# Row-wise division by the sum of absolute values: loads and stores of all tiles issued from one queue in a fixed order

## The chip, the cores and the metric

The kernel runs on one core of a Trainium2 chip. The metric is the time on the device in microseconds (us), the median of several executions of the same compiled program. The engines named here are VectorE (DVE in the profile), ScalarE (ACT), GpSimd (POOL) and SyncE (SP). SyncE does no arithmetic; it issues transfers (DMAs) and waits on semaphores. ScalarE computes and can issue transfers too. The transfers themselves are carried out by 16 DMA engines, whichever engine issued them.

## The reference

The input is a tensor of 32 x 512 x 1024 float32 numbers. Each row of 1024 is divided by the sum of its absolute values:

```python
def reference(x: np.ndarray) -> np.ndarray:
    sums = np.sum(np.abs(x), axis=-1, keepdims=True)
    return (x / (sums + 1e-8)).astype(np.float32)
```

There are 16384 rows, 67.11 MB in and the same amount out. No number is read twice and there is nothing for TensorE to do.

## The kernel before

The 16384 rows are spread over the 128 partitions of the on-chip memory, so each partition holds 128 rows in all. They are worked on in eleven tiles. Ten tiles have 12 rows in each partition (128 x 12 x 1024 numbers, 6.29 MB), and the last has 8 (4.19 MB). The list `rows` holds these sizes and `piece` gives the part of the input or output that belongs to a tile. A partition's share of a tile is contiguous in HBM, 48 KB for 12 rows and 32 KB for 8.

The tiles live in the pool `sbuf`, which has four buffers (`BUFS = 4`). Tile 4 goes into the buffer of tile 0, tile 5 into that of tile 1, and so on. The results are written over the input in the same buffer (`row` is both input and output), so a buffer is free for the next load only when the store of the tile that it held has landed.

For each tile, `normalize` does this:

- one reduction on DVE over the whole tile, giving 12 sums of absolute values for each partition (line 52);
- two small DVE instructions on these sums: adding a tiny constant (line 59) and the reciprocal (line 61);
- the scaling of the rows by the reciprocals. Most rows are scaled by one DVE multiplication (line 63). In the tiles named in the table `split`, some rows are scaled one at a time by DVE (line 70) or by ACT (line 73), to shorten the work on the first and the last tiles.

The order of the work is written out by hand: inside `tc.manual_schedule()` each engine executes its instructions in program order. The loop runs over the tiles, and for each it issues the load on SyncE's queue (line 88), the computation, and the store on ScalarE's queue (line 91). SyncE thus has only loads to issue. It runs ahead of the computation: the first four loads have free buffers and are issued at once, and each later load waits until the store of four tiles before has landed. ScalarE has only stores to issue, each as soon as both DVE and ACT are done with the tile. Loads and stores are therefore on two separate queues, and the DMA engines serve both at once.

Of the kernel before, what the change touches and what calls it, by code (L numbers as in the profile page):

```python
# [1 line left out]

# [4 lines left out]

FP32 = mybir.dt.float32
EPS = 1e-8


@with_exitstack
def kernel(
    ctx: ExitStack,
    tc: tile.TileContext,
    x: bass.AP,
    out: bass.AP,
):
    nc = tc.nc
    P = nc.NUM_PARTITIONS  # L20

    x_flat = x.flatten_outer_dims()
    out_flat = out.flatten_outer_dims()
    n, d = x_flat.shape

    R = 12
    BUFS = 4  # L30
    HEAD = 32
    per_partition = n // P
    assert n % P == 0 and (per_partition - HEAD) % R == 0
    rows = [R] * ((per_partition - HEAD) // R + 2) + [HEAD - 2 * R]

    def piece(flat, i):
        head = flat[: P * HEAD, :].rearrange("(p r) d -> p r d", p=P)
        if i < 2:
            return head[:, R * i : R * (i + 1), :]
        if i == len(rows) - 1:  # L40
            return head[:, 2 * R :, :]
        a = P * (HEAD + R * (i - 2))
        return flat[a : a + P * R, :].rearrange("(p r) d -> p r d", p=P)

    sbuf = ctx.enter_context(tc.tile_pool(name="sbuf", bufs=BUFS))
    stats = ctx.enter_context(tc.tile_pool(name="stats", bufs=len(rows)))

    def normalize(x_tile, k, kv, kt):


        s = stats.tile([P, R], FP32)
        nc.vector.tensor_reduce(  # L52
            out=s[:, :k],
            in_=x_tile[:, :k, :],
            axis=mybir.AxisListType.X,
            op=mybir.AluOpType.add,
            apply_absolute_value=True,
        )
        nc.vector.tensor_scalar_add(out=s[:, :k], in0=s[:, :k], scalar1=EPS)  # L59
        inv = stats.tile([P, R], FP32)  # L60
        nc.vector.reciprocal(out=inv[:, :k], in_=s[:, :k])  # L61
        if kv:
            nc.vector.tensor_mul(  # L63
                out=x_tile[:, :kv, :],
                in0=x_tile[:, :kv, :],
                in1=inv[:, :kv].unsqueeze(2).to_broadcast([P, kv, d]),
            )
        for r in range(kv, kv + kt):
            row = x_tile[:, r, :]
            nc.vector.tensor_scalar_mul(out=row, in0=row, scalar1=inv[:, r : r + 1])  # L70
        for r in range(kv + kt, k):
            row = x_tile[:, r, :]
            nc.scalar.activation(  # L73
                out=row,
                in_=row,
                func=mybir.ActivationFunctionType.Copy,
                scale=inv[:, r : r + 1],
            )

    last = len(rows) - 1
    split = {0: (3, 4), 1: (0, 3), 2: (0, 3), last - 1: (0, 2), last: (5, 3)}

    with tc.manual_schedule():
        for i, k in enumerate(rows):
            x_tile = sbuf.tile([P, R, d], FP32)
            nc.sync.dma_start(out=x_tile[:, :k, :], in_=piece(x_flat, i))  # L88
            kt, ks = split.get(i, (0, 0))
            normalize(x_tile, k, k - kt - ks, kt)  # L90
            nc.scalar.dma_start(out=piece(out_flat, i), in_=x_tile[:, :k, :])


# [1 line left out]
_INS = ['x']  # L95
_OUTS = [((32, 512, 1024), 'float32')]


# [23 lines left out]
```

## Time and profile before

| What | Value |
|---|---|
| median of three executions | 317.26 us (317.24 to 317.40) |
| span of the profiled execution, first to last instruction | 315.8 us |
| time outside the span, median less span | 1.46 us |
| moved by the DMA engines | 134.22 MB, 425 GB/s over the span |
| DVE busy | 261.2 us, 83% of the span |
| ACT busy | 17.4 us |
| loads, 12 rows | ten of 6144 KB, median 38.0 us from issue to landing |
| stores, 12 rows | ten of 6144 KB, median 47.4 us from issue to landing |

The profiled execution has no total time of its own beside the span on the page; what lies around the span is taken from the difference to the median of the executions without the profiler.

The page lists the busy time of each engine, the span in 40 slices, the DMA queues (q1 is SyncE's, with the loads; q10 is ScalarE's, with the stores), the chain of work that ended last, groups of instructions and the DMA issues. The busy share of the DMA engines is a mean over all 16. A view by windows gives the same numbers for any stretch of the span. In it a DMA packet counts wholly in the window in which it starts, so that in a window shorter than a packet the share can be over 1 or be 0; over long windows this evens out. A packet here is the share of one partition in one transfer: a transfer of 12 rows has 128 data packets of 48 KB, eight for each DMA engine, and each engine ends its part with one packet of a few bytes that counts up the semaphore.

### The profile page before, as it was taken

How to read it: one execution, taken by the hardware profiler on the slowest of the kernel's cores; microseconds unless marked ns; L12 is line 12 of the kernel's file. 1: busy time of each engine (PE TensorE's matmuls, PEld its weight loads, DVE VectorE, ACT ScalarE, POOL GpSimd, SP SyncE). 2: the span in 40 equal slices, each digit the busy share in tenths (PEclk: the TensorE clock that was granted, in tenths of full speed). 3: DMA queues.
4: the chain of work that ended last, by engine and by line, in shares of the span. 5: the costliest groups of instructions: out<-in, count | busy, mean ns of one | idle time of the engine just before them, and what ended most of it. 6: DMA issues, size and time to landing. Idle time of an engine off the chain costs nothing.

```text
span 315.8 us, 168 instructions
## 1 busy us (share of the span) xinstructions
DVE 261.2 (83%) x51; ACT 17.4 (6%) x16; POOL 0.2 (0%) x4
## 2 busy tenths in 40 slices
DVE  0079999999999999969996999799699969999200
ACT  0010404004000000000000000000000000201200
POOL 0000000000000000000000000000000000000000
DMA  8999999999999999999999999999999999999986
GB/s 324 473 398 448 448 361 430 405 486 405 405 486 405 405 486 411 423 467 405 448 436 411 479 405 411 473 417 405 473 417 411 467 413 450 421 442 423 473 374 282
DMA packets 3168, 134.22 MB, mean 425 GB/s; under 512 B 352, under 2 KB 352, under 8 KB 352
## 3 DMA queue, kind: packets, MB, share of 16 engines
q1 hardware_dynamic: 1584, 67.11, 49.8%
q10 hardware_dynamic: 1584, 67.11, 49.1%
HBM read 67.11 MB, written 67.11 MB: 425 GB/s over the span
## 4 chain that ended last, share of the span: by engine, by line
DVE 41%; DMA 33%; another core or an unknown queue 18%; issue 0%; SPq 0%; DVEq 0%
DVE s L52 23%; DMA x_tile<-in_x_dram 17%; DMA out_dram<-x_tile 16%; DVE x_tile L63 15%; DVE x_tile L70 1%; DVE inv L61 0%; DVE s L59 0%; SPq L88 0%; DVEq L117 0%
## 5 line engine op out<-in xcount | busy, mean ns | idle before, releaser
L52 DVE TENSOR_REDUCE s<-x_tile 128x12 f32<-128x12288 f32 (+1 forms) x11 | 138.2, 12561 | 31.5 <-DMA x_tile<-in_x_dram 31.5
L63 DVE TENSOR_TENSOR x_tile<-x_tile,inv 128x12288 f32<-128x12288 f32 (+3 forms) x10 | 113.6, 11358 | 0.5
L73 ACT ACTIVATE x_tile<-x_tile,inv 128x1024 f32<-128x1024 f32 x15 | 16.1, 1138 | 258.7 <-DVE inv L61 258.7
L70 DVE TENSOR_SCALAR x_tile<-x_tile,inv 128x1024 f32<-128x1024 f32 x8 | 5.5, 748 | 0.0
L61 DVE RECIPROCAL inv<-s 128x12 f32<-128x12 f32 (+1 forms) x11 | 2.5, 226 | 0.4
L73 ACT ACT_TABLE_LOAD x1 | 1.3, 1283 | 17.7 <-DMA x_tile<-in_x_dram 17.7
L59 DVE TENSOR_SCALAR s<-s 128x12 f32<-128x12 f32 (+1 forms) x11 | 1.9, 173 | 0.4
L106 POOL MEMSET const-bfloat16-1.0<- 128x1 bf16 x1 | 0.1, 102 | 0.0
L106 POOL MEMSET const-uint8-127<- 128x1 uint8 x1 | 0.1, 102 | 0.0
L106 POOL MEMSET const-float32-0.0<- 128x1 f32 x1 | 0.1, 99 | 0.2 <-issue 0.2
L106 POOL MEMSET const-float32-1.0<- 128x1 f32 x1 | 0.1, 99 | 0.0
## 6 DMA issues: line engine op xcount, KB each, us to landing
x_tile<-in_x_dram SPq DMA_DIRECT2D x10, 6144.0 KB, 38.0
out_dram<-x_tile ACTq DMA_DIRECT2D x10, 6144.0 KB, 47.4
x_tile<-in_x_dram SPq DMA_DIRECT2D x1, 4096.0 KB, 33.3
out_dram<-x_tile ACTq DMA_DIRECT2D x1, 4096.0 KB, 20.6
```

The lines of the kernel that those rows point to most:

```text
L52: nc.vector.tensor_reduce(out=s[:, :k], in_=x_tile[:, :k, :], axis=mybir.AxisListType.X, op=mybir.AluOpType.add, apply_absolute_value=True,)
L59: nc.vector.tensor_scalar_add(out=s[:, :k], in0=s[:, :k], scalar1=EPS)
L61: nc.vector.reciprocal(out=inv[:, :k], in_=s[:, :k])
L63: nc.vector.tensor_mul(out=x_tile[:, :kv, :], in0=x_tile[:, :kv, :], in1=inv[:, :kv].unsqueeze(2).to_broadcast([P, kv, d]),)
L70: nc.vector.tensor_scalar_mul(out=row, in0=row, scalar1=inv[:, r : r + 1])
L73: nc.scalar.activation(out=row, in_=row, func=mybir.ActivationFunctionType.Copy, scale=inv[:, r : r + 1],)
L106: nc = _bacc.Bacc("TRN2", target_bir_lowering=False, num_devices=1)
```

## The change

The stores move from ScalarE's queue to SyncE's, which now issues all 22 transfers. The order in which SyncE issues them is fixed by the program: the loads of tiles 0 to 3, the stores of tiles 0 and 1, the load of tile 4, the store of tile 2, the load of tile 5, and so on in turn, until the load of tile 10 and then the stores of tiles 8, 9 and 10. An instruction of this queue that has to wait holds up those behind it: a store waits for the computation of its tile, and a load waits for the store that frees its buffer. The tile sizes, the number of buffers, the instructions of `normalize`, their order on DVE and ACT and the bytes moved stay as they are.

```diff
     with tc.manual_schedule():
-        for i, k in enumerate(rows):
-            x_tile = sbuf.tile([P, R, d], FP32)
-            nc.sync.dma_start(out=x_tile[:, :k, :], in_=piece(x_flat, i))
-            kt, ks = split.get(i, (0, 0))
-            normalize(x_tile, k, k - kt - ks, kt)
-            nc.scalar.dma_start(out=piece(out_flat, i), in_=x_tile[:, :k, :])
+        for i in range(BUFS):
+            load(i)
+        compute(0)
+        store(0)
+        for i in range(1, n_tiles):
+            compute(i)
+            store(i)
+            if i - 1 + BUFS < n_tiles:
+                load(i - 1 + BUFS)
```

The functions it calls are new:

```diff
+    tiles = {}
+
+    def load(i):
+        x_tile = tiles[i] = sbuf.tile([P, R, d], FP32, name="x_tile")
+        nc.sync.dma_start(out=x_tile[:, : rows[i], :], in_=piece(x_flat, i))
+
+    def store(i):
+        nc.sync.dma_start(out=piece(out_flat, i), in_=tiles[i][:, : rows[i], :])
+
+    def compute(i):
+        k = rows[i]
+        kt, ks = split.get(i, (0, 0))
+        normalize(tiles[i], k, k - kt - ks, kt)
+
+    n_tiles = len(rows)
```

## The prediction

> **What bounds the kernel now.** I read the page from the top: span, busy times, the slices, then the DMA queues.
>
> ```profile
> span 315.8 us, 168 instructions
> DVE 261.2 (83%) x51; ACT 17.4 (6%) x16; POOL 0.2 (0%) x4
> ...
> DMA  8999999999999999999999999999999999999986
> ...
> DMA packets 3168, 134.22 MB, mean 425 GB/s; under 512 B 352, under 2 KB 352, under 8 KB 352
> ## 3 DMA queue, kind: packets, MB, share of 16 engines
> q1 hardware_dynamic: 1584, 67.11, 49.8%
> q10 hardware_dynamic: 1584, 67.11, 49.1%
> ```
>
> DVE has 54.6 us of idle time; the DMA engines have almost none: the two queues' shares add to 98.9% of the span. The bound is the 16 DMA engines, not DVE and not a wait. So the first question is whether they can run faster in any mix of work. I asked the view by windows for three stretches of 14.5 us: loads alone, loads and stores together, stores alone (the last load is due to have landed by 281.5, where the last reduction starts).
>
> ```profile
> core 0: us, DVE busy (x) ACT busy (x) POOL busy (x), PEclk, DMA share, GB/s
> 18.90:33.40 14.50, 14.40 (x4) 2.38 (x4) 0.00 (x0) 1.00 1.00 434
> 126.00:140.50 14.50, 12.21 (x1) 0.00 (x0) 0.00 (x0) 1.00 1.00 434
> 282.00:296.50 14.50, 11.90 (x8) 3.23 (x3) 0.00 (x0) 1.00 1.00 434
> ```
>
> All three read 434 GB/s at a share of 1.00: loads alone, stores alone and both at once run equally fast. The first window also crosses the boundary from the load of tile 1 to that of tile 2 (eight packets each, one after the other on one queue) with no loss. At 434 GB/s the 134.22 MB take 309.3 us of the 315.8. What is left, 6.5 us, is all that the DMA side has to give. It lies at the start, at one place early on, and at the end. The start and the early place:
>
> ```profile
> 0.00:1.50 1.50, 0.00 (x0) 0.00 (x0) 0.20 (x4) 1.00 0.00 0
> 1.50:2.00 0.50, 0.00 (x0) 0.00 (x0) 0.00 (x0) 1.00 4.42 1376
> ...
> 4.00:4.50 0.50, 0.00 (x0) 0.00 (x0) 0.00 (x0) 1.00 3.18 1376
> ```
>
> ```profile
> 38.00:39.00 1.00, 1.00 (x2) 0.00 (x0) 0.00 (x0) 1.00 1.71 737
> 39.00:40.00 1.00, 1.00 (x1) 0.00 (x0) 0.00 (x0) 1.00 0.11 49
> 40.00:41.00 1.00, 1.00 (x1) 0.00 (x0) 0.00 (x0) 1.00 3.08 786
> 41.00:42.00 1.00, 1.00 (x1) 0.00 (x0) 0.00 (x0) 1.00 0.00 0
> 42.00:43.00 1.00, 1.00 (x1) 0.00 (x0) 0.00 (x0) 1.00 0.00 0
> 43.00:44.00 1.00, 1.00 (x1) 0.00 (x0) 0.00 (x0) 1.00 1.70 737
> ```
>
> A packet counts where it starts. The window from 38 holds 737 GB/s x 1 us = 15 packets of 49152 bytes, so one takes 1.71 x 16 / 15 = 1.82 us, the normal packet. The window from 40 holds exactly 16 packets, one for each engine, and its share of 3.08 says that each took 3.08 us: 1.26 more than normal, on all engines. The first store was issued on ScalarE's queue at 38.67 (timeline), so this is what opening the second queue cost, once. No other full round of packets is stretched so. At the start, the first packets begin near 1.7: the window from 1.5 holds 1376 GB/s x 0.5 us = 14 of the 16, each of 4.42 x 0.5 x 16 / 14 = 2.5 us, 0.7 over normal. The account: 1.7 + 0.7 + 309.3 + 1.26 = 313.0, the mean end of the engines, and 2.8 us from there to the end of the span (the slowest engine ends about 1.4 after the mean, then the last landing and the closing semaphores).
>
> Last, the waits of SyncE and of DVE, to see what the changed order has to respect.
>
> ```profile
> SPq L88 <- DMA out_dram<-x_tile: 227.8, 7, 56.4
> ...
> DVE s L52 <- DMA x_tile<-in_x_dram: 31.5, 7, 17.6
> ```
>
> All seven later loads wait for a store to free a buffer; DVE waits 31.5 us for loads, 17.6 for the first. As the DMA engines are busy meanwhile, these waits cost nothing by themselves.
>
> **The change part by part.** Unchanged: every instruction of DVE and ACT, the bytes, and the start. The sum is made against the span of 315.8; the median is 1.46 above it, which I carry over.
>
> *Issuing.* Eleven stores leave ScalarE (0.34 us each) and are issued by SyncE beside its eleven loads (0.33 us): 22 x 0.33 = 7.3 us of issue time in 315, each while another transfer is running. At nothing, as long as the queue holds an earlier transfer for over 0.33 us. ACT's 16 instructions wait for DVE alone, so its lighter queue gains nothing.
>
> *One queue, in order.* A transfer of 12 rows takes 14.5 us of every engine alone (8 x 1.81), one of 8 rows 9.7. In order, with the first load done at 17, loads 1 to 3 end at 31.5, 46 and 60.5. The store of tile 0 is issued at 38.7 as now, but has loads 2 and 3 ahead of it: it runs 60.5 to 75, store 1 (issued 61.8) to 89.5. Load 4 waits for store 0, is issued at about 75.5 and runs 89.5 to 104. Then store 2 to 118.5, load 5 to 133, store 3 to 147.5, load 6 to 162, and in steps of 14.5 on: load 10 to 273, stores 8, 9 and 10 to 287.5, 302, 312. The question is whether each is issued in time. DVE, with 26.4 us for a full tile (12.95 + 0.4 + 12.96), ends tile 2 at 84.8 and tile 3 at 111.2 as now; load 4 is then in, so tile 4 ends at 137.6, 5 at 164, 6 at 190.5, 7 (its load in at 191) at 218, 8 (220) at 247, 9 (249) at 273.5, 10 at 287. Store 4 is issued at 137.7 and wanted at 162; store 6 at 190.5 and wanted at 220; store 10 at 287, wanted at 302. Load 4 is issued when store 0 ends, with store 1 (14.5 us) still in the queue; each later load has a load and a store ahead of it. The tightest cover is about 14 us (store 1, load 4, store 10); it would have to vanish wholly before an engine idles.
>
> *The new waits.* Behind a store that waits for DVE now stands a load. Load 7 needs store 3 (147.5); the store ahead of it, 4, is issued at 137.7. Loads 8, 9 and 10 have 12 to 16 us in hand in the same way (stores 4, 5 and 6 end at 176.5, 205.5 and 234.5; stores 5, 6 and 7 are issued at 164, 190.5 and 218), and store 5 (164) stands behind load 7 (148). Neither holds up the other. DVE waits some 1 to 2 us for each of loads 7 to 9, with over 15 us of transfers queued ahead of its stores, so at no cost.
>
> *The second queue is not opened.* The 1.26 us at 40 to 43 go if they belong to a queue that is opened while another runs; they stay if they belong to the first store as such. Between 0 and 1.26 I take the whole: from 43 on stores and loads alternate at 1.81 us a packet, so a change of direction has no price of this kind.
>
> *Changes of direction on one queue.* In one queue the order turns from loads to stores eight times and back seven times. No row shows this on one queue. From below: no gain, since no stage exceeds 434 GB/s. The nearest row for nothing is the mixed stretch, 434 GB/s with both directions on every engine. From above: 0.7 us for a packet on an empty pipeline (the start), or 1.26 (the opening): 15 x 0.7 = 10.5, 15 x 1.26 = 18.9. I take 0, because the mixed stretch has the same engines turning between packets, and differs only in which queue a packet comes from.
>
> *The end.* Stores 9 and 10 end alone in both kernels. In order, the engines may end closer together: after 14.5 us windows of loads they still start within about 0.5 us of one another, at the end they are some 1.4 apart. Between 0 and 1.4 I take 0.2.
>
> Sum: 315.8 - 1.26 - 0.2 = 314.3 of span, with 1.46 around it **315.8 us**.
>
> **Two rules of the Trainium skill.** The page "DMA: Bandwidth & Descriptors", section "Issuing engines are not separate DMA queues", says that all transfers share the same 16 engines and that several issuers only save issue time. By it alone the change is worth nothing, 317.26; the row at 40 to 43 adds a price for the second queue that the page does not have. The same page, section "Anatomy of one DMA" (for the GpSimd path), gives a fixed cost of about 2 us for each transfer, mostly the receipt of the last write. This speaks against the change: if one queue exposed it at each of 21 boundaries, the page's figure would make an estimate of 42 us more. The window of loads alone crosses such a boundary at 434 GB/s, so here it is overlapped.
>
> **The rivals.** *First, no change:* the 1.26 us belong to the first store after loads alone, and come again at 60. For it: it is seen once, at the first store, so the profile can't part the two. Against: later stores show nothing like it. Time: 317.26, less up to 0.2.
>
> *Second, slower: the turn between directions costs on one queue.* Place: the 15 turns. For it: with two queues an engine may fetch from one while it finishes the other; with one it has nothing else at the turn. Against: load follows load on one queue without a gap. Price: 0.7 each gives 317.26 - 1.26 + 10.5 = 326.5; 1.26 each gives 334.9; 0.4 each gives 322. It decides from (1.26 + 0.63) / 15 = 0.13 us a turn.
>
> *Third, the queue runs dry* because a waiting store or load stands in front. For it: SyncE's queue now mixes both waits. Against: 12 to 14 us of cover everywhere. One dry spell costs about 1.0 (issue at 0.73 to the first packet at 1.7) + 0.7; at seven loads 12 us, 328.
>
> **How the numbers follow.** What can be told from no change here is 0.2%, 0.63 us. Forecast 0.60; first rival 0.12; second 0.24; third 0.04. So faster 0.60, same 0.12, slower 0.28. The forecast's own range is 314.6 (the opening and the whole spread at the end gone: 317.26 - 1.26 - 1.4) to 316.6. The range with the others goes up to 322, the second rival at 0.4 a turn; small prices are likelier, so about half of that case, and all of the third, lie above: some 0.15 in all, with 0.03 below.
>
> **What the new profile would show.** Right: no round of 3.08 us packets near 40 or 60; one queue with some 99% of the span; 434 GB/s over windows that cross a turn (such as 82 to 111); loads landing 14 to 15 us after the transfer ahead; DVE idle moved, not gone. Wrong: packets longer than 1.82 us at each turn, at 60, 89.5, 104 and so on, or slices under 9 tenths in the middle. The prediction fails most simply if a turn on one queue costs more than 0.13 us.

## The result and the profile after

The changed kernel is slower: a median of 320.02 us (319.82 to 320.45, four runs) against 317.33 us for the kernel before beside it, a ratio of 1.0082 with a 95% interval of 1.0069 to 1.0096. I had forecast 315.8 us. The case that I had called the second rival, a cost at the turns between loads and stores on one queue, took place.

The page of the changed kernel, the lines that answer to those shown of before:

```profile
span 318.2 us, 159 instructions
DVE 261.1 (82%) x51; ACT 17.4 (5%) x16; POOL 0.2 (0%) x4
...
DMA  8999999999999999999999999999999999999994
...
DMA packets 3168, 134.22 MB, mean 422 GB/s; under 512 B 352, under 2 KB 352, under 8 KB 352
## 3 DMA queue, kind: packets, MB, share of 16 engines
q1 hardware_dynamic: 3168, 134.22, 98.3%
```

The same packets are all on one queue, the busy times of DVE and ACT are the same within 0.1 us, and no slice in the middle is under nine tenths. So no DMA engine ran dry for want of a transfer. The only slice that falls is the last, from 6 tenths to 4. Its rate on the page falls from 282 to 177 GB/s. The loss shows at the end of the span.

The waits of SyncE and of DVE:

```profile
SPq L86 <- DVE x_tile L58: 137.1, 9, 24.3
SPq L83 <- DMA out_dram<-x_tile: 93.9, 7, 17.1
...
DVE s L47 <- DMA x_tile<-in_x_dram: 28.5, 6, 17.7
```

SyncE now waits for computation and for stores, as the change says, and DVE waits for loads a little less than before (28.5 against 31.5 us). The waits are not what costs time.

The view by windows, with a packet counted where it starts, has three parts to look at. First the whole stretches, which answer to the 434 GB/s of before:

```profile
core 0: us, DVE busy (x) ACT busy (x) POOL busy (x), PEclk, DMA share, GB/s
62.00:76.50 14.50, 14.40 (x4) 1.36 (x2) 0.00 (x0) 1.00 1.00 434
82.00:111.00 29.00, 28.90 (x5) 0.00 (x0) 0.00 (x0) 1.00 1.00 432
111.00:140.00 29.00, 28.84 (x6) 0.00 (x0) 0.00 (x0) 1.00 1.00 431
140.00:169.00 29.00, 26.94 (x5) 0.00 (x0) 0.00 (x0) 1.00 1.00 432
```

Stores alone run at 434 GB/s as before. The windows that hold turns have 431 or 432 at a share of 1.00: the engines are busy, but some packets take longer. Now the first turn, from load 3 to store 0, and two packets at a later one:

```profile
58.00:59.00 1.00, 1.00 (x1) 0.00 (x0) 0.00 (x0) 1.00 2.48 688
59.00:60.00 1.00, 1.00 (x1) 0.00 (x0) 0.00 (x0) 1.00 0.36 98
60.00:61.00 1.00, 1.00 (x1) 0.00 (x0) 0.00 (x0) 1.00 0.00 0
61.00:62.00 1.00, 1.00 (x2) 0.00 (x0) 0.00 (x0) 1.00 1.71 737
...
191.50:192.30 0.80, 0.80 (x1) 0.00 (x0) 0.00 (x0) 1.00 1.54 614
```

The window from 58 holds 688 GB/s x 1 us = 14 packets, each of 2.48 x 16 / 14 = 2.83 us: the last packets of load 3, stretched by 1.0. The stretch that I had put down to the opening of the second queue is still there, 18 us later, at the first store to reach the engines. In the window from 191.5 there are 614 x 0.8 = 491 KB, ten packets, of mean 1.54 x 0.8 x 16 / 10 = 1.97 us. Two of them, on engines that are 1.3 and 1.8 us behind the median, take 2.57 and 2.59 us in the records of the packets; the other eight take the normal 1.82.

Last, the final packets of all engines, in the changed kernel and then in the kernel before:

```profile
312.00:313.00 1.00, 0.00 (x0) 0.00 (x0) 0.00 (x0) 1.00 0.53 229
313.00:314.00 1.00, 0.00 (x0) 0.00 (x0) 0.00 (x0) 1.00 0.23 98
314.00:315.00 1.00, 0.00 (x0) 0.00 (x0) 0.00 (x0) 1.00 0.23 98
315.00:316.00 1.00, 0.00 (x0) 0.00 (x0) 0.00 (x0) 1.00 0.23 98
```

```profile
312.00:313.00 1.00, 0.00 (x0) 0.00 (x0) 0.00 (x0) 1.00 0.46 197
313.00:314.00 1.00, 0.00 (x0) 0.00 (x0) 0.00 (x0) 1.00 0.16 66
314.00:315.00 1.00, 0.00 (x0) 0.00 (x0) 0.00 (x0) 1.00 0.00 0
```

These packets belong to tile 10, whose 8 rows make packets of 32 KB. Before, the last two (66 GB/s x 1 us) start between 313 and 314. After, three (98 GB/s x 1 us) still start in each microsecond up to 316. Three engines are late by some 3 us, and the kernel ends when the slowest does.

To find where these engines lost their time I joined the packets into one chain for each engine. The records don't name the engine, but a packet starts within a few nanoseconds of the end of the one before it, and eight data packets and one counting packet make up an engine's part of a transfer. Durations over the normal 1.82 us are the loss. The mean over the 16 engines in the changed kernel is 0.69 us at the start, 1.04 at the first turn (0.66 to 1.36), 0.78 at the last two packets of a load ahead of the seven later turns to a store, 0.15 at the first two packets of a load after a turn back, and nothing elsewhere. The slowest engine lost 3.06 us after the first turn. The mean end of the engines moved from 313.41 (before) to 313.96, the end of the slowest from 314.38 to 316.75. That is 2.37 us, and the span grew by 2.4. Most of the loss is thus in how far the engines end apart. The rest of this study asks what makes the late engines late.

### The profile page after: what moved, and what is told of

It reads as the page before. It is cut to its first block, busy times and chain, and to the rows that moved or that the text cites. A ratio compares the mean times of both kernels' runs of the same rounds, so it can differ in the third digit from the quotient of the medians.

```text
span 318.2 us, 159 instructions
## 1 busy us (share of the span) xinstructions
DVE 261.1 (82%) x51; ACT 17.4 (5%) x16; POOL 0.2 (0%) x4
## 4 chain that ended last, share of the span: by engine, by line
DMA 58%; DVE 33%; DVEq 0%; issue 0%; SPq 0%
DMA x_tile<-in_x_dram 32%; DMA out_dram<-x_tile 26%; DVE s L47 19%; DVE x_tile L58 12%; DVE x_tile L65 1%; DVE inv L56 0%; DVE s L54 0%; DVEq L129 0%; DVEq L58 0%; SPq L86 0%; SPq L83 0%
## 5 line engine op out<-in xcount | busy, mean ns | idle before, releaser
L47 DVE TENSOR_REDUCE s<-x_tile 128x12 f32<-128x12288 f32 (+1 forms) x11 | 138.2, 12561 | 28.5 <-DMA x_tile<-in_x_dram 28.5
```

The source lines that it names most:

```text
L47: nc.vector.tensor_reduce(out=s[:, :k], in_=x_tile[:, :k, :], axis=mybir.AxisListType.X, op=mybir.AluOpType.add, apply_absolute_value=True,)
```

## The experiments

All times are medians, and each ratio is to the kernel before on the same chip, with its 95% interval. The span and the end of the last engine are those of one profiled execution, which need not be like the median one.

| Kernel | queues | turns from loads to stores | time, us | ratio | span | last engine ends |
|---|---|---|---|---|---|---|
| before | 2 | packet by packet | 317.33 | 1 | 315.8 | 314.4 |
| changed | 1 | 8 | 320.02 | 1.0082 (1.0069 to 1.0096) | 318.2 | 316.8 |
| changed, again | 1 | 8 | 320.23 | 1.0089 (1.0074 to 1.0105) | 318.8 | 317.4 |
| pairs | 1 | 5 | 318.71 | 1.0043 (1.0027 to 1.0059) | 317.0 | 315.5 |
| stores on ScalarE | 2 | packet by packet | 317.07 | 0.9990 (0.9974 to 1.0007) | 315.0 | 313.6 |
| copy | 1 | 8 | 320.29 | 1.0091 (1.0060 to 1.0122) | 318.5 | 317.2 |
| copy, fours | 1 | 3 | 317.30 | 0.9994 (0.9976 to 1.0012) | 314.9 | 313.7 |
| copy, fours, eight engines late | 1 | 3 | 322.09 | 1.0157 (1.0143 to 1.0172) | 320.1 | 318.9 |
| halves | 1 | 8 | 320.12 | 1.0086 (1.0072 to 1.0099) | 318.0 | 316.6 |
| halves in turn | 1 | 15 | 321.87 | 1.0146 (1.0133 to 1.0159) | 319.8 | 318.4 |
| two engines late | 1 | 8 | 321.93 | 1.0142 (1.0128 to 1.0157) | 319.6 | 318.0 |
| early store | 2 | packet by packet | 317.54 | 1.0006 (0.9994 to 1.0017) | 315.0 | 313.7 |
| flat, two queues | 2 | packet by packet | 318.14 | 1.0025 (1.0009 to 1.0042) | 318.4 | 317.0 |
| flat, one queue | 1 | 8 | 320.69 | 1.0105 (1.0092 to 1.0118) | 319.2 | 317.8 |

The theory at first: on one queue, an engine that turns from a load to a store loses time, the late engines most. The rivals were the order of issue (not the queue), the waits for DVE and its traffic, and a lag that has nothing to do with turns.

### Fewer turns: pairs

```diff
-        compute(0)
-        store(0)
-        for i in range(1, n_tiles):
-            compute(i)
-            store(i)
-            if i - 1 + BUFS < n_tiles:
-                load(i - 1 + BUFS)
+        for i in range(0, last, 2):
+            compute(i)
+            store(i)
+            compute(i + 1)
+            store(i + 1)
+            for j in (i + BUFS, i + 1 + BUFS):
+                if j <= last:
+                    load(j)
+        compute(last)
+        store(last)
```

> All transfers stay on SyncE's queue, but the loads and stores after the first four loads go in pairs (two stores, two loads), so that the queue turns from loads to stores five times instead of eight, and back four times instead of seven. Turn theory (a DMA engine that turns from a load to a store on one queue loses time, the late engines most): the first turn still costs about 1.0 us on all engines, the later loss of the slowest engine (about 3.5 us in the changed kernel) shrinks to about 4/7 of it, 2.0, so 318.5 us. Rival, lag from something that does not depend on turns (number of loads, number of transfers): 320.0 as before.

318.71 us, close to the 318.5 of the turn theory, and its interval excludes the time of the changed kernel. The number of transfers, their sizes and the work are the same; only the order differs. The slowest engine lost 2.38 us after the first turn, against 3.06.

### The queue alone: stores on ScalarE

```diff
     def store(i):
-        nc.sync.dma_start(out=piece(out_flat, i), in_=tiles[i][:, : rows[i], :])
+        nc.scalar.dma_start(out=piece(out_flat, i), in_=tiles[i][:, : rows[i], :])
```

> The program order of the changed kernel is kept, only the stores go back to ScalarE's queue. Turn theory: 317.3 us, with the engines ending about 1.4 us apart. Rival, the order of issue is to blame and not the single queue: about 320.

317.07 us: with the program order of the changed kernel, and only the queue of the stores put back, the whole loss is gone. The engines end within 0.74 us of each other, closer than I expected. The order of issue by itself is out.

### No computation: copy

```diff
     def compute(i):
-        k = rows[i]
-        kt, ks = split.get(i, (0, 0))
-        normalize(tiles[i], k, k - kt - ks, kt)
+        pass
```

> The same queue and the same order of the 22 transfers as in the changed kernel, with the whole computation left out: the output is a copy of the input. Turn theory: the loss lies in the DMA engines alone, so the time stays near 320.0 (319 to 321) and stretched last packets of loads appear before every turn to a store. Rival, the waits of SyncE for DVE or the traffic of DVE and ACT in the on-chip memory cause the loss: 316.0 to 317.0, with no stretched packets after the first turn.

320.29 us, as the turn theory has it. DVE and ACT do nothing here, and SyncE waits for transfers alone, so neither their traffic nor their lateness is the cause. The loss lies in the transfers themselves.

### Fewest turns: copy in fours

```diff
-        for i in range(BUFS):
-            load(i)
...
+        for g in range(0, n_tiles, BUFS):
+            group = range(g, min(g + BUFS, n_tiles))
+            for i in group:
+                load(i)
+            for i in group:
+                store(i)
```

> As the copy, with the computation left out, but four loads and four stores in turn, so that the queue turns three times from loads to stores and twice back. Turn theory: time below the other copy by about 5/7 of the 3.5 us lost after the first turn, so about 317.5. If every turn of engines that are in step costs 1 us like the first one: three rounds of packets of about 2.8 us on all engines. Rival, turns do not matter: the same time as the other copy within 0.6.

317.30 us against 317.5 expected: 3.0 below the other copy, with all bytes on one queue. In this copy, one queue as such costs nothing, then; the turns do. In its windows, the first turn and the second:

```profile
58.00:59.00 1.00, 0.00 (x0) 1.00 2.54 737
59.00:60.00 1.00, 0.00 (x0) 1.00 0.18 49
...
172.90:174.70 1.80, 0.00 (x0) 1.00 1.01 437
174.70:176.50 1.80, 0.00 (x0) 1.00 1.01 437
```

(There is no column for DVE or ACT here.) At 58, 15 packets take 2.54 x 16 / 15 = 2.71 us. Load 7 gives way to store 4 just after 176, and its last packets start in the last window. Each window of 1.80 us holds exactly 16 packets of 1.82 us: this turn is free for all engines, which are then within 0.6 us of one another. So a turn has no fixed price. The first one is a case of its own.

### What does a turn cost, and whom?

In the two profiles of the changed kernel I compared, at the seven later turns from loads to stores, how far an engine was behind the median and what it lost on its last two load packets:

| behind the median by | cases | mean loss | share that lost over 0.1 us |
|---|---|---|---|
| under 0.3 us | 158 | 0.04 us | 16% |
| 0.3 to 1 us | 32 | 0.21 us | 66% |
| over 1 us | 34 | 0.45 us | 85% |

The copy (0.04, 0.18 and 0.41 us) and the pairs (0.05, 0.13 and 0.51 us) agree. Being late goes with being delayed further, and so a few engines fall behind more and more. The table alone can't tell whether being late delays an engine, or whether some engines are slow anyway and are late for that reason. The next experiment was meant to show that lateness is the cause. Ahead of everything it loads eight partitions once more, which gives eight engines one packet more; tile 3 then follows whole, into the same buffer.

```diff
+        tiles[3] = sbuf.tile([P, R, d], FP32, name="x_tile")
+        nc.sync.dma_start(out=tiles[3][:8, :, :], in_=piece(x_flat, 3)[:8, :, :])
...
```

> The copy in groups of four, with one transfer more at the very start: eight partitions of tile 3, 48 KB each, which go to eight of the 16 DMA engines and put them one packet (1.81 us) behind the others; the computation is left out. In the copy in groups of four the second turn from loads to stores, near 174, stretched no packet on any engine (all within 0.6 us of one another). Lag theory (a late engine loses time when the others have already turned): the eight late engines now lose 0.3 to 0.8 us each at the turns near 175 and 274, and the time is 317.3 + 1.8 + 0.6 to 1.6 = 319.7 to 320.7. Rival, every turn has a price of its own, or some engines are slow whatever their lag: no stretch at 175, and 317.3 + 1.8 = 319.1 or less.

322.09 us, over both expectations, and for a reason that neither had. From its windows:

```profile
1.50:2.50 1.00, 0.00 (x0) 1.00 2.93 393
3.00:4.00 1.00, 0.00 (x0) 1.00 2.86 393
...
62.20:64.00 1.80, 0.00 (x0) 1.00 1.01 437
...
64.00:65.80 1.80, 0.00 (x0) 1.00 1.01 437
```

The first packets took 5.9 us (2.93 x 16 / 8) and 5.7 us instead of 2.5, on all 16 engines, over 3 us longer. The first turn, near 65, then cost nothing on any engine, unlike in every other run. And at the second turn, near 182, the late engines (1.2 to 1.9 us behind the others) lost nothing. They lost 0 to 0.28 us at the third, where the largest loss, 0.50 us, fell on an engine that was not late. The lag theory failed here: being late is not enough.

I repeated it in the order of the changed kernel, with its computation, and with only two engines made late.

```diff
+        tiles[3] = sbuf.tile([P, R, d], FP32, name="x_tile")
+        nc.sync.dma_start(out=tiles[3][:2, :, :], in_=piece(x_flat, 3)[:2, :, :])
...
```

> The changed kernel with one small transfer more at the start: two partitions of tile 3, 48 KB each, which put two of the 16 DMA engines one packet (1.8 us) behind. Lag theory: the two late engines are stretched by 0.3 to 0.8 us at most of the turns to stores, as late engines are in the changed kernel, and end 2 to 4 us beyond their extra packet, 321.5 to 323.5 us. Rival, the loss at a turn does not depend on being late: the two lose no more than the median engine, and the time is 320 to 320.5, or set by the two at 313.9 + 1.8 in the span.

321.93 us, within the lag theory's range. The windows of the last packets:

```profile
313.00:314.00 1.00, 0.00 (x0) 0.00 (x0) 0.00 (x0) 1.00 0.31 131
314.00:315.00 1.00, 0.00 (x0) 0.00 (x0) 0.00 (x0) 1.00 0.23 98
315.00:316.00 1.00, 0.00 (x0) 0.00 (x0) 0.00 (x0) 1.00 0.15 66
316.00:317.00 1.00, 0.00 (x0) 0.00 (x0) 0.00 (x0) 1.00 0.15 66
```

In the joined chains, the two engines with the additional packet can be told by it. They end last, at 318.03 and 317.61. Each lost 1.5 us after the first turn, less than the 2 to 4 expected; the median of the other 14 lost 0.1, although two of these lost 1.7 and 2.1. So in this order both engines that were made late were delayed further, but two that were not made late lost more. In groups of four with half of the engines late, the late ones were hardly delayed. That lateness is the cause is not shown, and what separates the two runs is open.

### More turns: halves, and halves in turn

Each transfer is split into two of 6 rows, in the control one right after the other, and then alternating. The diff is that of the second kernel against the control.

```diff
-            for step, t in ((store_half, i), (load_half, j)):
-                for h in (0, 1):
+            for h in (0, 1):
+                for step, t in ((store_half, i), (load_half, j)):
                     if t < n_tiles:
                         step(t, h)
```

> The changed kernel with each transfer split into two of 6 rows, one right after the other, so that there are 44 transfers and as many turns as before. It is the control for the next kernel. Any theory in which turns or lag decide: 320.0 within 1. If each transfer as such costs something: more, by 22 times the price.

> As the control with halves, but the halves of a store and of the following load alternate, so that the queue turns from loads to stores 15 times instead of 8, in steps of 7.25 us. Turn theory (a price for each turn): about 3.5 us after the first turn become 14/7 of it, so 323 us. Lag theory with a loss that depends on how far engines are apart: also more, 321 to 323, as there are more occasions. Rival, only the length of the one-way stretches matters and finer mixing approaches the two queues: 318 or less.

The control takes 320.12 us: 22 transfers more cost nothing that can be seen. With 15 turns it takes 321.87, 1.75 us more, and the intervals of the two don't overlap. The turn theory has the right direction again, but had 323: against the 317.30 of the kernel before, about twice the turns give 4.6 us of loss instead of 2.8, not twice as much. Over all kernels, 3, 5, 8 and 15 turns give 317.3 (the copy), 318.7, 320.1 and 321.9 us. Finer mixing on one queue did not approach the two queues.

### What is the stretch at the first store?

It is there on two queues (1.26 us) and on one (1.04). Three tries at its cause. The first puts a small store ahead of everything, on two queues.

```diff
+    first = stats.tile([P, 128], FP32)
...
+        nc.gpsimd.memset(first[:, :], 0.0)
+        nc.scalar.dma_start(out=piece(out_flat, last)[:, 0, :128], in_=first[:, :])
```

> The kernel before, with two queues, and one small store ahead of everything on ScalarE's queue: 512 bytes of each partition of the last tile's output, zeros, overwritten at the end by the real store. If the stretch of about 1.2 us at 40 is the price of the first store whatever its size and time: it comes near 3 us instead, no packets of 3 us at 40, and the time is the same within 0.6 or better by up to 1.2 us (316.1) if it is hidden at the start. If it belongs to the first full stores beside loads alone: it stays at 40, 317.3 to 317.6.

317.54 us, no difference, and the stretch stays in its place, as the windows show:

```profile
40.00:41.50 1.50, 1.50 (x1) 0.00 (x0) 0.00 (x0) 1.00 2.00 524
41.50:43.50 2.00, 2.00 (x1) 0.00 (x0) 0.00 (x0) 1.00 0.00 0
```

These are 16 packets of 2.00 x 1.5 = 3.0 us. So neither the first write of any size nor the first use of ScalarE's queue is what costs.

The other two take all tiles in order from the flat tensor, so that tiles 0, 1 and 10 are no longer read and written with a step of 128 KB from one partition to the next.

```diff
-        head = flat[: P * HEAD, :].rearrange("(p r) d -> p r d", p=P)
...
-        a = P * (HEAD + R * (i - 2))
-        return flat[a : a + P * R, :].rearrange("(p r) d -> p r d", p=P)
+        a = P * R * i
+        return flat[a : a + P * rows[i], :].rearrange("(p r) d -> p r d", p=P)
```

> The kernel before, on two queues, with all tiles taken in order from the flat tensor, so that tiles 0, 1 and 10 also have a step of 48 or 32 KB from partition to partition instead of 128 KB. If the stretches of 0.7 us at the start and 1.2 us at the first store come from the step of 128 KB, on which all engines start at once: both are gone or halved, 315.5 to 316.5 us. If they belong to a start from rest and to the first store as such: 317.3, stretches as before.

> The changed kernel, on one queue, with the same flat tiles. If the step of 128 KB matters at the first turn (load 3 to store 0), the 1.0 us at 58 are gone and the late engines have less of a start: 318 to 319.3. If not: 320.0.

318.14 and 320.69 us: no gain on either, and on two queues a small loss. The stretches at the first store stay, 1.15 and 1.12 us in the mean. The step of 128 KB is out, too. Since the first turn was free in the run with the slow first packets, the cause of this stretch is open.

The last packets of the flat kernel on two queues show something else:

```profile
313.00:314.00 1.00, 0.00 (x0) 0.00 (x0) 0.00 (x0) 1.00 0.23 98
314.00:315.00 1.00, 0.00 (x0) 0.00 (x0) 0.00 (x0) 1.00 0.15 66
315.00:316.00 1.00, 0.00 (x0) 0.00 (x0) 0.00 (x0) 1.00 0.08 33
```

Its last engine ends at 316.98, 3.2 us after the mean of the engines (313.76), although loads and stores are on two queues. Its twelve executions took 317.08 to 320.02 us, and the profiled one is the slowest. In the records of its packets, 14 load packets from 46 us on are stretched by over 0.06 us, the most by 0.65 us, and one packet of a store by 0.11. The profile of the kernel before has ten such load packets (0.12 to 0.42 us), that of the kernel with the stores on ScalarE none. So stretched load packets and late engines occur on two queues as well, in some executions: of 29 executions of the kernel before beside the pairs, one took 319.82 us.

### Once more

The changed kernel was run again for a second profile.

> The changed kernel itself once more, for a second profile on this chip: 320.0 us, and stretched last packets of loads at the turns to stores again. Lag theory: the engines that end last are again those that were behind after the first turns, not a fixed set.

320.23 us, with stretched packets at the same turns. The slowest engine lost 4.06 us after the first turn. Whether the same engines are late each time can't be told, since the records don't name them.

No kernel tried is faster than the one before beyond its interval.

## Why the prediction was wrong, point by point

**The bound and the cover: right.** The DMA engines bound both kernels. The worked-out queue held: load 4 was issued at 77.19 (75.5 forecast), store 4 at 137.63 (137.7), load 7 at 150.81 (148), and no DMA engine waited for a transfer. DVE waited 2.7 to 3.0 us for each of loads 7 to 9, where I had 1 to 2, and this cost nothing either. The third rival, a queue that runs dry, did not occur. The new waits of SyncE cost nothing, nor did issuing 22 transfers from it.

**"The second queue is not opened", -1.26: wrong.** The term goes with the first full store, not with the queue, in all kernels but the one with the slow first packets. It came back as 1.04 us at 58 to 60 on the one queue. The first rival had named this; the profile of before could not part the two, and I gave it 0.12.

**"Changes of direction on one queue", 0: wrong, and the step that turned the sign.** I argued that the mixed stretch, 434 GB/s with both directions on every engine, has the same turns. The difference that I called "only in which queue a packet comes from" was the point. The same program with the stores on the other queue takes 317.07 us, and the fewer the turns on one queue, the less the loss. The mean loss is small: 0.78 + 0.15 = 0.93 us for an engine over the 14 turns after the first, under 0.07 a turn. My bounds (0 to 18.9) held it, and by the mean alone the change would have been within 0.6 us of no change. The range with all rivals, 314.6 to 322, holds the 320.02 us too, but only by the second rival; the direction that I forecast was wrong.

**"The end", -0.2: wrong, in sign and size.** I set it between 0 and 1.4 of gain and never asked whether the engines could end further apart. The slowest ended 1.0 us after the mean before (I had read 1.4, which is how far the first and the last are apart), and 2.8 us after it in the changed kernel: +1.8. This is three quarters of the loss of 2.4 us in the span. What I missed is that a cost at a turn need not be equal on all engines, and that 16 engines that each do a fixed share end with the slowest. The slowest lost 3.06 us over 14 turns, 0.22 a turn, over the 0.13 at which I had this rival decide.

**The rule of the Trainium skill.** The page "DMA: Bandwidth & Descriptors", section "Rules for kernel authors", says that spreading transfers over several issuing engines does not help bandwidth, only issue time. Here two kernels that differ only in the queue of the stores take 320.0 and 317.1 us, 0.9%, with issue time hidden in both; the measurement decides. The section "Queues, rings and completion order" says that an engine serves its queues in turn, a packet from each, where a packet is a group of descriptors, typically some 9 to 17. The trace of before agrees as to the turns: from 43 on, while both queues have work, records of 48 KB from the two queues alternate on each engine at 1.82 us each. How many descriptors make up a record, no run here shows.

**What is shown and what is argued.** Shown: with loads and stores in turn on one queue, all eight executions of the changed kernel took 319.61 to 321.03 us; the loss went when the stores alone moved to the other queue; it grows with the number of turns, needs no computation, and sits mostly in the last packets of loads and on late engines. One queue is not a condition for it: the flat kernel on two queues had late engines too in its profiled execution, and the median of that kernel is 318.14 us. In these runs the second queue made them rarer. Not shown: that lateness is the cause and not some engines that are slow anyway, what in the engine or the memory stretches these packets, and why some turns are free. One can argue that two queues let an engine work on the other direction while a load's last packet waits; no run looked at that directly.

## What to carry to other kernels

Where the DMA engines are the bound, keep loads and stores on two queues, worth 0.8 to 0.9% here. Letting one queue turn rarely may do as well: in groups of four, one queue was as fast as two, but this was tried only in a copy without computation. Price an edit of the transfer order by the slowest of the engines, not by their mean; look at the last microseconds of the span and at how far apart the final packets start. When one row of the trace allows two readings, as the stretch at the first store did, the better term is the range over both and not the larger gain.

## What the runs showed of the hardware that I had not expected

An engine that is late at a turn from loads to stores tends to be delayed further in the changed kernel: 0.04 us when under 0.3 us behind, 0.45 when over 1 us behind. The loss falls on the last load packets before the turn; a turn back costs a few engines 0.1 to 0.5 us on the second packet. In the two profiles of the changed kernel, packets of stores kept their 1.82 us within 0.01 us. One additional transfer on eight partitions at the very start stretched the first packets of all 16 engines from 2.5 us to between 5.5 and 6.2. The stretch of about 1 us at the first full store is there on one queue and on two, with and without computation, and was missing only after that slow start. Splitting 22 transfers into 44 had no cost that can be seen (320.12 against 320.02 us), and packets at the boundary of two loads are as long as any other.
